# Layer 0's first MLP product as seven block products, its result by way of DRAM

## The chip, the cores and the metric

The kernel runs on one core of a Trainium2 chip. A core has five engines with instruction streams of their own: TensorE (PE; its weight loads are listed apart as PEld), VectorE (DVE), ScalarE (ACT), GpSimd (POOL) and SyncE (SP), which here only issues transfers. The metric is the device time of one execution in microseconds (us), lower is better.

## The reference, cut to what matters

Two layers run over 512 latent tokens and 256 context tokens of width 1024, all in float32. Per layer:

```
u   = modulate(rmsnorm(x, norm1_w), sh1, sc1)
z   = split(u @ w_in)                       # 5888 columns: retention, attention, pooling, gates
mix = merge_branches(retention, pooling, attention, gates, ...) @ w_out
x   = x + g1 * mix
x   = x + g2 * (square(relu(modulate(rmsnorm(x, norm2_w), sh2, sc2) @ w_mlp1)) @ w_mlp2)

pooling: mixed = einsum('blgc,gcd->blgd', window_means - ug, w_grp) * scale     # 4 groups of 128 channels
```

`w_mlp1` is 1024 x 4096, `w_mlp2` 4096 x 1024. Layer 0 computes all 768 tokens (6 tiles of 128), the last layer only the 512 latent ones after its projections.

## The kernel before, in words

**Products.** Each float32 operand is split into a high part (rounded to float32r by a ScalarE copy) and a low part (the rest, by a subtraction on VectorE or GpSimd). `mm3` (L302 to L305) then issues three matmuls: high x high, high x low, low x high. Almost all TensorE work goes through these three lines, so the profile's groups are told apart by the tile that they write: `tg` (projections, output projection, last MLP chunks), `pg` (gates), `pb` (branches), `pu` (pooling projection), `pp` (pooling mix), `ph` (first MLP product), `st` (second MLP product).

**Weights.** The class `Weights` holds one plan of slots in the order of their use. `next` hands out slot i, issues the loads of slot i+3 on SP's queue (L109) and enters the split of slot i+2 in a list; `tick`, called between matmuls, takes one piece of 512 columns from that list (L139 on ScalarE, L140 on VectorE or GpSimd). There are six raw buffers and three pairs of split ones. `combine` (L152) adds or subtracts two raw blocks on GpSimd, for the second MLP product.

**Order.** Work is written as generators that are interleaved by hand: a `Filler` gives out so many estimated microseconds of matmuls between the steps of a chain of dependent work. A scheduler then orders each engine's instructions by a simulated time line, so that a ready instruction can go ahead of an earlier one that waits. Large tiles (12 KB a partition) come from one pool, `big`, of 11 buffers.

**Layer 0 in time.** From 0 to some 150 us: modulation weights, norm, and the first projections (`T1`: pairs of 256 columns, moving operand 256 wide). To 320 us: the other projections (`T2`) as filler beside retention and the query and key norms; the four pooling groups come last. Each group's `pu` is evicted to `up` (one buffer), VectorE adds shifted copies (`ps`), forms `pd`, and the mixing matmul `pp` (`mixed`, L693) is issued after the next group's first eviction; the result goes to `pm`. To 620 us: attention, with the gates and branches 0 and 1 as filler; `to_hilo_feat` splits `pm` before branch 1. To 759 us: branch 2 and the output projection, in two groups of tiles, (0,1,2,3) and (4,5), each followed by its part of the second norm. To 1290 us: the MLP, with layer 1's modulation products between.

**The MLP.** The 4096 hidden columns are 8 chunks of 512. The first product of a chunk (`mlp1`, L1244) runs slab by slab of 128 hidden columns, moving 512 and then 256 tokens, 8 k-tiles x 3 matmuls each; ScalarE makes relu and square in place (L1263, L1264). Chunks 0 to 5 then go through `strassen` (L1169), the second product as seven block products of 2 x 2 blocks (Strassen-Winograd): VectorE forms sums of blocks of the hidden state (L1191), ScalarE and VectorE split them (L1195, L1196), and each of the 21 banks of a chunk is added to the sums `acc` (L1225; in chunk 0 twelve of them are copied by ScalarE). The order is m1 0, then m1 c and s2 c-1 in turn, s2 5, `fold`, m1 6, m1 7, and `m2` for chunks 6 and 7 in the ordinary way:

```python
            o = [("m1", 0)]
            for ch in range(1, NSC):
                o += [("m1", ch), ("s2", ch - 1)]
            o += [("s2", NSC - 1), ("fold",), ("m1", 6), ("m1", 7)]
```

Layer 1 has the same form with 512 tokens.

## Time and profile before

| | |
|---|---|
| median of 3 runs | 2161.41 us (2160.17 to 2162.72) |
| profiled execution | 2159.42 us, of it 2157.6 us from the first to the last instruction |
| TensorE busy, mean granted clock | 2091.7 us (97%), 0.992 |
| VectorE, ScalarE, GpSimd busy | 1323.2, 860.0, 614.9 us |
| read from and written to memory | 216.27 MB, 7.37 MB |

The trace is of one execution. A matmul's duration in it reaches past the start of the next one, since they are pipelined; starts show the rate. A window's row gives each engine's busy time in a stretch, with the number of instructions in brackets.

### The profile page before, as it was taken

What the parts mean: (1) busy time and instruction counts of PE and PEld (TensorE: products, weight loads), DVE (VectorE), ACT (ScalarE), POOL (GpSimd) and SP (SyncE); (2) the same over time, 40 slices, a digit from 0 to 9 for tenths busy, and PEclk for the clock granted to TensorE, in tenths of its full rate; (3) what the DMA queues carried; (4) which work ended last, traced back from release to release, by engine and by line L of the source; (5) the groups of instructions that cost most, each with busy time, mean ns of one, the idle gap of its engine ahead of it and who ended that gap; (6) DMA issues with size and microseconds to landing.
All of it is one profiled execution on the core that took longest, in us unless ns stands there. A gap on an engine that the chain in (4) does not pass through costs nothing.

```text
span 2157.6 us, 33841 instructions
## 1 busy us (share of the span) xinstructions
PE 2091.7 (97%) x13407; PEld 1803.8 (84%) x13407; DVE 1323.2 (61%) x2523; ACT 860.0 (40%) x1707; POOL 614.9 (29%) x481
## 2 busy tenths in 40 slices
PE   5999989999999999999999999998999999999999
PEld 5999968888888788888888889996888888887787
DVE  4597973454543654446569557479455367778884
ACT  3323423443432354434343335233454445654441
POOL 0242242222223331232222224333333353212300
PEclk8999999999999999999999999999999999999999
DMA  9751111111124534244426243211222164233241
GB/s 314 241 174 40 41 38 55 50 40 50 40 59 161 155 135 146 91 135 128 139 96 206 69 146 101 79 46 51 74 61 77 54 209 128 88 98 111 80 132 49
DMA packets 224598, 225.83 MB, mean 105 GB/s; under 512 B 8320, under 2 KB 180664, under 8 KB 224440
## 3 DMA queue, kind: packets, MB, share of 16 engines
q1 hardware_dynamic: 208744, 168.96, 25.3%
q0 software_dynamic: 15696, 54.71, 7.3%
q8 instruction: 105, 1.72, 0.3%
q14 instruction: 53, 0.43, 0.1%
HBM read 216.27 MB, written 7.37 MB: 104 GB/s over the span
## 4 chain that ended last, share of the span: by engine, by line
PE 81%; DVE 13%; issue 2%; ACT 2%; DMA 1%; POOL 0%; SPq 0%; DVEq 0%; ACTq 0%; POOLq 0%
PE ph L303 7%; PE ph L304 7%; PE ph L305 7%; PE tg L304 5%; PE tg L303 5%; PE tg L305 5%; PE pg L303 5%; PE pg L305 5%; PE pg L304 5%; PE st L303 4%; PE st L304 3%; PE st L305 3%; PE pb L304 3%; PE pb L303 3%; PE pb L305 3%; PE m L1099 2%
## 5 line engine op out<-in xcount | busy, mean ns | idle before, releaser
L140 POOL TENSOR_TENSOR wl<-wr,wh 128x512 fp32r<-128x512 f32 x304 | 415.2, 1379 | 938.8 <-ACT wh L139 904.3
L139 ACT ACTIVATE wh<-wr 128x512 fp32r<-128x512 f32 x640 | 370.6, 623 | 556.8 <-issue 222.1
L140 DVE TENSOR_TENSOR wl<-wr,wh 128x512 fp32r<-128x512 f32 x336 | 238.1, 731 | 254.9 <-ACT wh L139 254.8
L304 PE MATMUL ph<-u2l,wh 128*128 128x512 f32 (+1 forms) x808 | 278.9, 346 | 1.3 <-DVE u2l L1379 1.3
L303 PE MATMUL ph<-u2h,wh 128*128 128x512 f32 (+1 forms) x808 | 279.3, 348 | 0.3 <-ACT wh L139 0.3
L305 PE MATMUL ph<-u2h,wl 128*128 128x512 f32 (+1 forms) x808 | 277.4, 345 | 0.0
L303 PE MATMUL tg<-wh,uh 128*128 128x256 f32 x784 | 226.6, 289 | 1.0 <-ACT uh L1378 0.9
L304 PE MATMUL tg<-wl,uh 128*128 128x256 f32 x784 | 223.7, 285 | 1.6 <-POOL wl L140 1.6
L305 PE MATMUL tg<-wh,ul 128*128 128x256 f32 x784 | 222.6, 285 | 0.0
L303 PE MATMUL pg<-uh,wh 128*128 128x512 f32 (+1 forms) x576 | 208.4, 362 | 0.0
L304 PE MATMUL pg<-ul,wh 128*128 128x512 f32 (+1 forms) x576 | 207.1, 360 | 0.0
L305 PE MATMUL pg<-uh,wl 128*128 128x512 f32 (+1 forms) x576 | 207.1, 359 | 0.0
L152 POOL TENSOR_TENSOR wr<-wr,wr 128x1024 f32<-128x1024 f32 x48 | 116.7, 2430 | 259.1 <-DVE wl L140 220.0
L303 PEld LDWEIGHTS ph<-u2h,wh 128*128 128x128 f32 x808 | 152.1, 189 | 22.4 <-issue 2.8
L303 PE MATMUL st<-wh,ob 128*128 128x512 f32 x420 | 165.6, 398 | 5.1 <-DVE acc L1225 2.9
L304 PEld LDWEIGHTS ph<-u2l,wh 128*128 128x128 f32 x808 | 153.0, 189 | 19.9 <-DVE u2l L1379 1.7
L305 PEld LDWEIGHTS ph<-u2h,wl 128*128 128x128 f32 x808 | 152.8, 189 | 18.7
L304 PE MATMUL st<-wl,ob 128*128 128x512 f32 x420 | 165.2, 393 | 1.1 <-DVE wl L140 1.1
L305 PE MATMUL st<-wh,ob 128*128 128x512 f32 x420 | 164.7, 392 | 0.0
L303 PEld LDWEIGHTS tg<-wh,uh 128*128 128x128 f32 x784 | 150.8, 192 | 3.5 <-issue 1.8
L304 PEld LDWEIGHTS tg<-wl,uh 128*128 128x128 f32 x784 | 150.9, 193 | 2.7 <-POOL wl L140 2.0
L305 PEld LDWEIGHTS tg<-wh,ul 128*128 128x128 f32 x784 | 150.3, 192 | 1.3 <-issue 1.2
(316 smaller groups left out, 4160.4 us busy)
## 6 DMA issues: line engine op xcount, KB each, us to landing
wr<-in_w_mlp_dram SPq DMA_DIRECT2D x136, 512.0 KB, 4.2
wr<-in_w_in_dram SPq DMA_DIRECT2D x88, 512.0 KB, 3.8
adaw<-in_ada_w_dram POOLq DMA_DIRECT2D x42, 1024.0 KB, 6.1
wr<-in_w_out_dram SPq DMA_DIRECT2D x32, 512.0 KB, 3.9
adaw<-in_ada_w_dram SPq DMA_DIRECT2D x6, 1024.0 KB, 18.2
wr<-in_w_ret_out_dram SPq DMA_DIRECT2D x16, 256.0 KB, 2.8
wr<-in_w_pool_out_dram SPq DMA_DIRECT2D x16, 256.0 KB, 2.8
wr<-in_w_attn_out_dram SPq DMA_DIRECT2D x32, 128.0 KB, 3.0
```

What stands on the lines that cost most here:

```text
L139: A.activation(out=box["h"][:, a:b], in_=r[:, a:b], func=AF.Copy)
L140: eng.tensor_tensor(out=box["l"][:, a:b], in0=r[:, a:b], in1=box["h"][:, a:b].bitcast(F32), op=ALU.subtract)
L152: nc.gpsimd.tensor_tensor(out=t, in0=self.raw[a], in1=self.raw[b], op=f)
L303: T.matmul(ps, ah, bh, start=first, stop=False, **kw)
L304: T.matmul(ps, ah, bl, start=False, stop=False, **kw)
L305: T.matmul(ps, al, bh, start=False, stop=last, **kw)
L1099: T.matmul(m2[KV[v], 2, :], vt[:, b, 64 * v : 64 * v + 64], PT[:, v, i, :], start=(i == 0), stop=(i == nb - 1), tile_position=(0, 64 * v), ...
```

## The change

In layer 0 (`SA`), the first MLP product of all eight chunks becomes seven block products as well (`s1`): weights in blocks of 512 rows x 256 columns, tokens in halves of 384, so 4 k-tiles x 2 slabs x 3 matmuls of 384 columns for each product. The seven operands of the token side (`operands`) are formed once and kept in seven large tiles; the weight blocks' sums are formed on GpSimd in halves. Each chunk's hidden state is written to DRAM and read back for the second product, whose six chunks now follow all eight first products; chunks 6 and 7 are split when they come back (`split67`). The output projection of layer 0 goes in groups of three tiles.

The first projections (`t_wide`) put two neighbouring blocks of 256 columns beside each other, moving 512 columns. The pooling mix leaves the projection stage: VectorE writes `pd`'s values to `pm`, and `mix_gen` runs the mixing matmuls between branches 0 and 1 and splits their result; layer 0's groups go from the widest window to the narrowest; the first gate takes the place at the end of the projection stage. Layer 1 has the changes of projection and pooling, not that of the MLP. The core of the diff:

```diff
+    class Beside(tuple):
+        def __new__(cls, whole, parts):
+            t = super().__new__(cls, (whole,))
+            t.parts = parts
+            return t
...
+            if isinstance(src, Beside):
+                for q, sq in enumerate(src.parts):
+                    nc.sync.dma_start(out=r[:, :].rearrange("p (k b n) -> p k b n", k=k, b=2)[:, :, q, :], in_=sq)
+                self.raw[name] = r
+                return
...
+                for op in pre[1] if pre is not None else ():
+                    self.bg.append((i, lambda op=op: self.combine(*op)))
-                eng = V if key[0] == "s2" or key[0] in ("m1", "m2") and not (key[0] == "m1" and key[1:3] == (1, 0) and key[3] > 1) or key[:2] == ("t", 0) and key[2] < C_AK else nc.gpsimd
+                eng = V if key[0] in ("s1", "s2") or key[0] in ("m1", "m2") and not (key[0] == "m1" and key[1:3] == (1, 0) and key[3] > 1) or key[:2] == ("t", 0) and key[2] < C_AK else nc.gpsimd
+                half = key[0] == "out" or key[0] in ("m1", "m2") and key[1] == 0 or key[:3] == ("t", 0, C_RV + 256) or key[0] == "s1" and key[3] > 1
...
+        def combine(self, o, a, b, f, oo=0, ao=0, bo=0, n=1024):
+            if o not in self.raw:
+                self.raw[o] = wp.tile([P, 1024], F32, name=f"wr{self.nr}", tag="raw", bufs=6)
+                self.nr += 1
+            nc.gpsimd.tensor_tensor(out=self.raw[o][:, oo : oo + n], in0=self.raw[a][:, ao : ao + n], in1=self.raw[b][:, bo : bo + n], op=f)
...
-    T2 = ((C_RG, C_RG + 256, C_AK, C_AQ, C_AQ + 256, 0, 1, 2, 3), (C_RG, C_RG + 256, C_AK, 3, 2, C_AQ, C_AQ + 256, 1, 0))
+    T2 = ((C_RG, C_RG + 256, C_AK, C_AQ, C_AQ + 256, 3, 2, 1, 0), (C_RG, C_RG + 256, C_AK, 3, 2, C_AQ, C_AQ + 256, 1, 0))
...
+    ON = (((0, 1, 2), (3, 4, 5)) if 0 in SA else NG[0], NG[1])
...
+        if l in SA:
+            o = [("s1", ch) for ch in range(8)] + [("s2", ch) for ch in range(NSC - 1)] + [("h67",), ("s2", NSC - 1), ("fold",)]
+            return o + [("m2", 6, g) for g in (NG[0] if l == 0 else mlp2_groups(l, 6))]
...
-            kp = t1_kper(l, pr)
-            for s in range(KT // kp):
-                for cb in pr:
-                    W.add(("t", l, cb, s), wslab(w_in[l], s * kp * P, kp, cb, 256))
+            for s in range(KT // 2):
+                q = [wslab(w_in[l], s * 256, 2, cb, 256) for cb in pr]
+                W.add(("t", l, pr[0], s), Beside(wslab(w_in[l], s * 256, 2, 0, 512), q))
...
+            if o[0] == "s1":
+                slab = [wslab(w_mlp1[l], 0, 8, o[1] * CHUNK + j * P, P) for j in range(4)]
+                r0, r1, ra = ([(l, o[1], n, q) for q in range(2)] for n in ("r0", "r1", "ra"))
+                add, sub = ALU.add, ALU.subtract
+                for q in range(2):
+                    W.add(("s1", l, o[1], q), slab[0], ([(r0[q], slab[2 * q])], []), parts=((r0[q], 0), (r0[q], 512)))
+                for q in range(2):
+                    ops = [(ra[q], r1[q], r1[q], add, 0, 0, 512, 512), (ra[q], ra[q], r0[q], sub, 512, 0, 0, 512)]
+                    W.add(("s1", l, o[1], 2 + q), slab[0], ([(r1[q], slab[2 * q + 1])], ops), parts=((ra[q], 0), (ra[q], 512)))
+                for q in range(2):
+                    ops = [(r1[q], r0[q], r1[q], sub, 0, 0, 0, 512), (r0[q], r0[q], ra[q], sub, 512, 512, 512, 512)]
+                    W.add(("s1", l, o[1], 4 + q), slab[0], ([], ops), parts=((r1[q], 0), (r0[q], 512)))
+                W.add(("s1", l, o[1], 6), slab[0], ([], []), parts=((r1[0], 512), (r1[1], 512)))
...
+        def t_wide(pr):
+            short = [t for t in alltiles if pr[1] >= C_RQ and t not in tiles]
+            banks = {}
+            sv = [store(dsts[cb]) for cb in pr]
+            for s in range(KT // 2):
+                wh, wl = W.next(("t", l, pr[0], s))
+                for t in alltiles:
+                    n = 256 if t in short else 512
+                    o = 256 * short.index(t) if t in short else 0
+                    key = -1 if t in short else t
+                    if key not in banks:
+                        banks[key] = ps.tile([P, 512], F32, name=f"tw{t}", tag="g")
+                    for k in range(2):
+                        kk = 2 * s + k
+                        tt = slice(t * P, (t + 1) * P)
+                        mm3(banks[key][:, o : o + n], xh(kk)[:, tt], xl(kk)[:, tt], wh[:, k, :n], wl[:, k, :n],
+                            first=(kk == 0 and o == 0), last=(kk == KT - 1), skip_group_check=True)
+                    if 2 * s + 2 == KT:
+                        if t not in short:
+                            for q in range(2):
+                                sv[q](banks[t][:, 256 * q : 256 * q + 256], [t])
+                        elif t == short[-1]:
+                            sv[0](banks[-1], short)
+                    W.tick()
+                    yield 2 * 3 * n / 2400.0
+
+        f1 = Filler(chainup(*[t_wide(pr) for pr in T1]))
...
-                d = wk.tile([P, 800], F32, name=f"pd{g}", tag=f"pls{(g + 1) % 2}")
-                V.scalar_tensor_tensor(out=d[:, 8:e], in0=src[:, 8:e], scalar=1.0 / w, in1=up[:, 8:e], op0=ALU.mult, op1=ALU.subtract)
...
+                    d = pm[:, g, t0 : t0 + n]
+                    V.scalar_tensor_tensor(out=d, in0=src[:, o : o + n], scalar=1.0 / w, in1=up[:, o : o + n], op0=ALU.mult, op1=ALU.subtract)
...
-                def mixed(g=g, d=d, pw=pw):
-                    for t0, n in groups:
-                        o = 8 if t0 == 0 else 536
-                        pp = ps.tile([P, 512], F32, name=f"pp{g}{t0}", tag="r")
-                        T.matmul(pp[:, :n], pw, d[:, o : o + n], start=True, stop=True)
-                        A.activation(out=pm[:, g, t0 : t0 + n], in_=pp[:, :n], func=AF.Copy, scale=wcol[l][:, 64 + g : 65 + g])
-                pend.append(mixed)
...
-            while pend:
-                pend.pop(0)()
+            y_tile()
+            yield from gate(0, 0, y_part(0))
...
+        pw = wkt.tile([P, 4, P], F32, name=f"pw{l}", tag="th")
+        nc.gpsimd.dma_start(out=pw, in_=pool_w[l].rearrange("g k d -> k g d"))
+
+        def mix_gen():
+            bh, bl = hl["p"] = bigt(f"bph{l}", F32R), bigt(f"bpl{l}", F32R)
+            for g in range(4):
+                sc = wcol[l][:, 64 + g : 65 + g]
+                for t0, n in groups:
+                    pp = ps.tile([P, 512], F32, name=f"pp{g}{t0}", tag="g")
+                    T.matmul(pp[:, :n], pw[:, g, :], pm[:, g, t0 : t0 + n], start=True, stop=True)
+                    h = bh[:, g, t0 : t0 + n]
+                    A.activation(out=h, in_=pp[:, :n], func=AF.Copy, scale=sc)
+                    V.scalar_tensor_tensor(out=bl[:, g, t0 : t0 + n], in0=pp[:, :n], scalar=sc, in1=h.bitcast(F32), op0=ALU.mult, op1=ALU.subtract)
+                    yield 4 * n / 2400.0
...
+                elif b == 0:
+                    ths = y_part(ft)
+                    if ft:
+                        yield from gate(b, ft, ths)
...
-        f3 = Filler(chainup(branch_gen(0, lambda: hl["r"]), branch_gen(1, lambda: to_hilo_feat(pm, "bp")), gate2_gen()))
+        f3 = Filler(chainup(branch_gen(0, lambda: hl["r"]), mix_gen(), branch_gen(1, lambda: hl["p"]), gate2_gen()))
...
+        def operands(part):
+            ublk = lambda kh, th: u2h[kh][:, :, th * HT : th * HT + HT]
+            b11, b12, b21, b22 = (ublk(kh, th) for kh in range(2) for th in range(2))
+            for pq, blk, sm in ((1, b11, None), (2, b21, None)) if part == 0 else (
+                    (5, b11, (b12, b11)), (6, b11, (b22, b11)), (7, b12, (b22, b12)), (3, b22, None), (4, b21, (b21, b11))):
+                o = big.tile([P, 2, 4, HT], F32R, name=f"ub{l}{pq}", tag="big")
+                ub[pq] = o
+                for k in (slice(0, 2), slice(2, 4)):
+                    if sm:
+                        V.tensor_tensor(out=blk[:, k], in0=sm[0][:, k], in1=sm[1][:, k], op=ALU.subtract)
+                    A.activation(out=o[:, 0, k], in_=blk[:, k], func=AF.Copy)
+                    V.tensor_tensor(out=o[:, 1, k], in0=blk[:, k], in1=o[:, 0, k].bitcast(F32), op=ALU.subtract)
+
+        hd = [tc.dram_tile([P, 4 * ntok], F32, name=f"hd{l}{ch}") for ch in range(8)] if sa else None
+
+        def s1(ch):
+            ht = big.tile([P, 4, ntok], F32, name=f"ht{l}{ch}", tag="big")
+            banks = {}
+            seq = [[(1, 0), (2, 0)], [(1, 1), (2, 1)], [(5, 0), (6, 0)], [(5, 1), (6, 1)], [(7, 0), (3, 0)], [(7, 1), (3, 1)], [(4, 0), (4, 1)]]
+            for e, prods in enumerate(seq):
+                wh, wl = W.next(("s1", l, ch, e))
+                for hf, (pq, q) in enumerate(prods):
+                    key = {1: "x", 6: "x", 7: "x", 4: "x", 5: "y", 3: "y", 2: "z"}[pq], q
+                    new = key not in banks
+                    if new:
+                        banks[key] = ps.tile([P, 512], F32, name=f"sp{l}{ch}{pq}{q}", tag="g")
+                    bk = banks[key][:, :HT]
+                    for k in range(4):
+                        mm3(bk, wh[:, 4 * hf + k, :], wl[:, 4 * hf + k, :], ub[pq][:, 0, k], ub[pq][:, 1, k], new and k == 0, k == 3, skip_group_check=True)
+                        if k % 2:
+                            W.tick()
+                    f, th = {1: (0, 0), 2: (0, 0), 5: (1, 1), 6: (0, 1), 7: (1, 1), 3: (0, 1), 4: (1, 0)}[pq]
+                    hv = ht[:, 2 * q + f, th * HT : th * HT + HT]
+                    if pq in (1, 5, 6, 4):
+                        A.activation(out=hv, in_=bk, func=AF.Copy)
+                    else:
+                        V.tensor_tensor(out=hv, in0=bk, in1=hv, op=ALU.add)
+                    if pq in (3, 4):
+                        hf2 = ht[:, 2 * q + f, :]
+                        V.scalar_tensor_tensor(out=hf2, in0=hf2, scalar=0.0, in1=hf2, op0=ALU.max, op1=ALU.mult)
+                    yield 4 * 3 * HT / 2400.0
+                if ch == 0 and e == 1:
+                    yield None
+            nc.sync.dma_start(out=hd[ch], in_=ht.rearrange("p a b -> p (a b)"))
+
+        def load_h(ch):
+            if sa and ch not in hs:
+                hs[ch] = big.tile([P, 4, ntok], F32, name=f"hr{l}{ch}", tag="big")
+                nc.sync.dma_start(out=hs[ch].rearrange("p a b -> p (a b)"), in_=hd[ch])
+
+        def split67():
+            for ch in (6, 7):
+                load_h(ch)
+            for ch in (6, 7):
+                r = hs[ch]
+                hh, hl_ = bigt(f"hh{l}{ch}", F32R), bigt(f"hl{l}{ch}", F32R)
+                hs[ch] = (hh, hl_)
+                for j in range(4):
+                    A.activation(out=hh[:, j, :ntok], in_=r[:, j, :], func=AF.Copy)
+                    V.tensor_tensor(out=hl_[:, j, :ntok], in0=r[:, j, :], in1=hh[:, j, :ntok].bitcast(F32), op=ALU.subtract)
+                    yield 0.0
 
         def strassen(ch):
+            if sa:
+                load_h(ch)
+                load_h(ch + 1)
...
-        for q, gr in enumerate(NG[l]):
+        for q, gr in enumerate(ON[l]):
             for cb in range(2):
                 for _ in t_gemm(("out", l, gr, cb), yhk, ylk, KT, 2, 512, gr, ps, "g", resid(g1, cb)):
                     pass
             if q == 1:
                 early()
             norm_group(gr, [xr[t // 3][:, t % 3, :] for t in gr], cl[:, 3], cl[:, 2], u2h, u2l, wk, ps, "t")
-        early()
+            if sa:
+                operands(q)
+        if not sa:
+            early()
...
-        for i in range(0, len(ts), 2):
+        for i, j in ((0, 1), (1, 3)) if ts == (3, 4, 5) else [(i, i + 2) for i in range(0, len(ts), 2)]:
...
             for q in range(4):
-                norm_mod(ts[i : i + 2], xns[i : i + 2], q, a, sh, uh, ul, wk, psp, tag)
+                norm_mod(ts[i:j], xns[i:j], q, a, sh, uh, ul, wk, psp, tag)
```

## Rows read from the trace of the kernel before

**Rows 1.** The page: busy us, share and instructions of each engine

```profile
PE 2091.7 (97%) x13407; PEld 1803.8 (84%) x13407; DVE 1323.2 (61%) x2523; ACT 860.0 (40%) x1707; POOL 614.9 (29%) x481
```

**Rows 2.** Windows: length, busy us of PE, PEld, DVE, ACT, POOL, clock, DMA, GB/s

```profile
0.00:60.00 60.00, 37.21 (x331) 32.81 (x332) 24.26 (x93) 23.08 (x39) 4.98 (x10) 0.89 0.92 308
...
110.00:160.00 50.00, 48.48 (x572) 46.65 (x565) 46.10 (x87) 10.51 (x21) 23.62 (x27) 1.00 0.52 171
...
770.00:1200.00 430.00, 430.00 (x2899) 362.74 (x2898) 254.53 (x355) 173.24 (x314) 118.34 (x89) 1.00 0.40 129
```

**Rows 3.** Waits of PE: total us, times, longest

```profile
PE pp L697 <- DVE pd L691: 9.1, 2, 8.1
PE pp L697 <- issue: 7.9, 1, 7.9
...
PE st L303 <- DVE acc L1225: 2.9, 4, 0.8
...
PE pp L697 <- DVE qsT L761: 1.2, 1, 1.2
```

**Rows 4.** Timeline of PE, 259 to 267 us: start, us, instruction, tiles, shapes

```profile
259.22 0.40 PE L303 MATMUL pu<-uh,wh 128*128 128x512 f32 x1
...
263.76 0.39 PE L305 MATMUL pu<-uh,wl 128*128 128x512 f32 x1
...
264.10 0.28 PE L304 MATMUL pu<-ul,wh 128*128 128x256 f32 x1
...
266.74 0.28 PE L305 MATMUL pu<-uh,wl 128*128 128x256 f32 x1
```

**Rows 5.** PE groups by shape: busy us, mean ns, idle before

```profile
L303 PE MATMUL ph<-u2h,wh 128*128 128x512 f32 x472 | 185.2, 392 | 0.3 <-ACT wh L139 0.3
...
L304 PE MATMUL ph<-u2l,wh 128*128 128x256 f32 x336 | 94.9, 284 | 1.3 <-DVE u2l L1379 1.3
```

**Rows 6.** Timeline of DVE, 1137 to 1169 us

```profile
1151.78 0.94 DVE L1196 TENSOR_TENSOR ob<-hb,ob 128x768 fp32r<-128x768 f32 x1
1152.64 1.28 DVE L140 TENSOR_TENSOR wl<-wr,wh 128x512 fp32r<-128x512 f32 x2
1153.85 1.87 DVE L1225 TENSOR_TENSOR acc<-st,acc 128x512 f32<-128x512 f32 x3
```

**Rows 7.** POOL groups by shape, 800 to 1200 us

```profile
L152 POOL TENSOR_TENSOR wr<-wr,wr 128x1024 f32<-128x1024 f32 x23 | 55.7, 2421 | 88.7 <-DVE wl L140 53.4 <-issue 34.6
```

**Rows 8.** DMA issues, 770 to 1200 us: count, KB each, median us to landing

```profile
xq<-xk SPq DMA_DIRECT2D x6, 512.0 KB, 7.0
```

**Rows 9.** DVE groups by shape, 800 to 1200 us

```profile
L1196 DVE TENSOR_TENSOR ob<-hb,ob 128x768 fp32r<-128x768 f32 x24 | 25.8, 1077 | 18.6 <-ACT ob L1195 18.6
L1196 DVE TENSOR_TENSOR ob<-stt,ob 128x768 fp32r<-128x768 f32 x18 | 23.4, 1301 | 16.2 <-ACT ob L1195 16.1
```

**Rows 10.** Window of the `st` tile alone: PE, PEld, DVE, ACT, clock, DMA

```profile
1105.70:1169.00 63.30, 58.98 (x252) 46.48 (x252) 25.69 (x39) 0.00 (x0) 1.00 0.58 183
```

**Rows 11.** Windows of all engines in second-product stretches, layer 0 and layer 1

```profile
1137.00:1169.00 32.00, 32.00 (x201) 25.76 (x200) 31.97 (x44) 10.94 (x19) 8.57 (x9) 1.00 0.80 247
2018.70:2041.00 22.30, 18.38 (x76) 13.62 (x75) 21.71 (x28) 12.35 (x22) 7.92 (x3) 0.97 0.07 26
```

**Rows 12.** Timeline of DVE, 705 to 785 us, around the second norm

```profile
763.61 0.68 DVE L1154 TENSOR_TENSOR xr<-xr,rt 128x512 f32<-128x512 f32 x1
...
779.93 1.29 DVE L1379 TENSOR_TENSOR u2l<-un,u2h 128x512 fp32r<-128x512 f32 x2 [1.16 <-ACT u2h L1378]
```

**Rows 13.** Timeline of DVE, 255 to 300 us

```profile
281.03 6.49 DVE L840 TENSOR_TENSOR aq<-aq,ropeA 128x512 f32<-128x512 f32 x1
...
291.75 0.68 DVE L840 TENSOR_TENSOR aq<-aq,ropeA 128x512 f32<-128x512 f32 x1
```

**Rows 14.** Windows of all engines behind two waits for `pp`

```profile
296.00:303.00 7.00, 7.00 (x24) 4.95 (x23) 4.37 (x10) 2.23 (x5) 1.83 (x2) 0.79 0.16 47
...
1497.00:1510.00 13.00, 13.00 (x48) 9.51 (x47) 12.79 (x22) 2.56 (x5) 3.17 (x3) 0.87 0.14 40
```

More of the change, by code (lines that the diff above doesn't have):

```diff
@@ L193, in bslab @@
         return (v[0], v[1])
-    def t1_kper(l, pr):
-        return 2 if l == 0 and pr == T1[0] else 4
     def tslots(l, key, cb, kh):
@@ L240 @@
                 W.add(("br", l, b, ft), bslab(l, b, ft))
-        for gr in NG[l]:
+        for gr in ON[l]:
             for cb in range(2):
@@ L255 @@
                                           (4, [], (t4, b21, t2, sub), t4)):
-                    W.add(("s2", l, o[1], pq), q[0][0], (loads, op), of)
+                    W.add(("s2", l, o[1], pq), q[0][0], (loads, [op] if op else []), of)
             elif o[0] == "m1":
@@ L598, in layer @@
         alltiles = list(range(NT))
-        def tspec(cb, dst):
-            return (("t", l, cb), tiles if cb >= C_RQ else alltiles, store(dst))
         def tcol(cb, dst):
-            return t_multi([tspec(cb, dst)], xh, xl, KT, 4, 256, ps, "g")
+            return t_multi([(("t", l, cb), tiles if cb >= C_RQ else alltiles, store(dst))], xh, xl, KT, 4, 256, ps, "g")
         def rope_ret(dst):
@@ L652, in pool_gen @@
                 up = wk.tile([P, 800], F32, name=f"up{g}", tag="up", bufs=1)
-                pw = wk.tile([P, P], F32, name=f"pw{g}", tag="pw", bufs=2)
-                nc.gpsimd.dma_start(out=pw, in_=pool_w[l, g])
                 V.memset(up[:, 0:8], 0.0)
-                e = 520 if last else 792
                 V.memset(up[:, 520:536], 0.0)
@@ L910, in post_gen, with gate, y_tile, y_part @@
             yield from norm_q()
+        def gate(b, ft, ths):
+            gh, gl = W.next(("gate", l, b, ft))
+            for (t0, n), th in zip(groups, ths):
+                pg = ps.tile([P, 512], F32, name=f"pg{ft}{t0}", tag="g")
+                for k in range(KT):
+                    mm3(pg[:, :n], gh[:, k, :], gl[:, k, :], xh(k)[:, t0 : t0 + n], xl(k)[:, t0 : t0 + n], k == 0, k == KT - 1)
+                    if k % 4 == 3:
+                        W.tick()
+                        yield 4 * 3 * n / 2400.0
+                A.activation(out=th, in_=pg[:, :n], func=AF.Tanh, scale=0.5)
+        y = []
+        def y_tile():
+            y.append(bigt(f"y{l}{len(y)}"))
+        def y_part(ft):
+            return [y[ft // 4][:, ft % 4, t0 : t0 + n] for t0, n in groups]
         marks = set()
@@ L943, in layer @@
         wk = es.enter_context(tc.tile_pool(name=f"wk_a{l}", bufs=2, reuse_waits="tile"))
-        def to_hilo_feat(src, nm):
-            bh, bl = bigt(f"{nm}h{l}", F32R), bigt(f"{nm}l{l}", F32R)
-            for k in range(4):
-                A.activation(out=bh[:, k, :ntok], in_=src[:, k, :ntok], func=AF.Copy)
-                V.tensor_tensor(out=bl[:, k, :ntok], in0=src[:, k, :ntok], in1=bh[:, k, :ntok].bitcast(F32), op=ALU.subtract)
-            return bh, bl
+        pw = wkt.tile([P, 4, P], F32, name=f"pw{l}", tag="th")
[11 more added lines that the diff above has]
+                    yield 4 * n / 2400.0
         def to_hilo_att(nm):
@@ L959, in to_hilo_att @@
             return bh, bl
-        y = [bigt(f"y{l}{q}") for q in range(2)]
-        def gate(b, ft, ths):
-            gh, gl = W.next(("gate", l, b, ft))
-            for (t0, n), th in zip(groups, ths):
-                pg = ps.tile([P, 512], F32, name=f"pg{ft}{t0}", tag="g")
-                for k in range(KT):
-                    mm3(pg[:, :n], gh[:, k, :], gl[:, k, :], xh(k)[:, t0 : t0 + n], xl(k)[:, t0 : t0 + n], k == 0, k == KT - 1)
-                    if k % 4 == 3:
-                        W.tick()
-                        yield 4 * 3 * n / 2400.0
-                A.activation(out=th, in_=pg[:, :n], func=AF.Tanh, scale=0.5)
+        y_tile()
         th2 = []
@@ L1158, in layer @@
         ylk = lambda k: yl[k // 4][:, k % 4, :]
-        u2h = [bigt(f"u2h{l}{q}", F32R) for q in range(2)]
-        u2l = [bigt(f"u2l{l}{q}", F32R) for q in range(2)]
+        sa = l in SA
+        if sa:
+            u2h, u2l = [bigt(f"uf{l}{q}") for q in range(2)], None
+        else:
+            u2h = [bigt(f"u2h{l}{q}", F32R) for q in range(2)]
+            u2l = [bigt(f"u2l{l}{q}", F32R) for q in range(2)]
         u2hk = lambda k: u2h[k // 4][:, k % 4, :]
@@ L1293, in mlp_gen @@
                     yield from strassen(o[1])
+                elif o[0] == "s1":
+                    yield from s1(o[1])
+                elif o[0] == "h67":
+                    yield from split67()
                 elif o[0] == "fold":
```

66 lines of the change are left out of this document (31 added, 35 removed).

## The prediction

> **What bounds the kernel now.** I read the engine totals first: TensorE is busy 97% of the span, VectorE 61% [rows 1]. So only work taken from TensorE, or a stall of it, can shorten the time; then the stretches by window say where that holds. In layer 0's MLP (770 to 1200 us) TensorE is busy 430.00 of 430 us at full clock while VectorE has 254.5 [rows 2]: each product removed there is time gained, as long as nothing else becomes the bound. Before that, from 110 to 160 us, VectorE is busy 46.1 of 50 [rows 2], so TensorE time saved there is worth less. The list of what TensorE waits for is short, and the pooling product `pp` leads it: 9.1 us on VectorE's `pd`, 7.9 us on "issue" [rows 3].
>
> A matmul's price is the spacing of starts, not its printed duration, since matmuls overlap. Twenty 512-column matmuls after the one at 259.22 another starts at 263.76: 0.227 us each; twenty-two after 264.10 one starts at 266.74: 0.120 us for 256 columns [rows 4].
>
> **First MLP product of layer 0.** The groups of `ph` matmuls [rows 5] hold both layers. By the code, layer 0 has 720 matmuls of 512 columns and 864 of 256 (the first two slabs of chunk 0 go in three pieces of 256): 720 x 0.227 + 864 x 0.120 = 267.1 us. After: 8 chunks x 7 products x 2 slabs x 4 k-tiles x 3 = 1344 matmuls of 384 columns. No row has that width; it costs at least 0.120 and at most 0.227 [rows 4], and I take the middle, 0.1735, since 256 columns more cost 0.107: 233.2 us. **-33.9 us**; the two ends (161 and 305 us) would need a price that is not linear, so I keep 0.170 (three quarters of 0.227) to 0.180 for the range, -38.6 to -25.2. The Trainium skill ("TensorE: Matmul & The Clock Gate", Back-to-back issue gap) gives columns over 2.4 GHz plus 2.5 ns; by it the saving would be an estimated 31.3 us, 2.6 less, but its 215.8 ns for 512 columns is below the 227 here.
>
> Who else works during it, per chunk of 168 x 0.1735 = 29.1 us: VectorE 9 halves of weight splits and 6 evictions at 0.60, 4 squared ReLUs of 768 elements at 0.86 [rows 6] = 12.4 us; GpSimd 8 combinations of 512 (half of the 2.42 of a 1024 one [rows 7]) and 5 split halves, some 16 us. Neither bounds. The hidden state goes out over SP's queue, 1.5 MB a chunk, three times a 512 KB transfer that lands in 7.0 us when queued with others [rows 8]; weight loads queue behind it. Slots run three loads ahead, so I charge only **+2 us** for seven chunk ends (range 0 to 20).
>
> **Second product, now six chunks in a row.** This is the part that gives time back. A Strassen chunk of the second product in layer 0 has 126 matmuls of 512 columns: 28.6 us. VectorE does 21 evictions and 14 split halves at 0.60 (three evictions in 1.87 us, the last one 0.67 long) and 11 operations on 768 elements at 0.86 (1151.78 to 1152.64) [rows 6]: 30.5 us; the 768 ones average 1.08 and 1.30 rather than 0.94 [rows 9], about 0.23 each lost, so 33.1. Before, each such chunk stood beside a first-product chunk that needed VectorE little. Where two stood back to back (252 matmuls in 63.30 us, 31.65 a chunk [rows 10]), VectorE was busy 31.97 of the last 32 us and TensorE just kept up [rows 11]; in layer 1, whose second-product chunks are smaller, two in a row do stop TensorE: 18.38 of 22.30 us [rows 11], waiting for `acc` [rows 3]. The 31.65 are 3.0 above 28.6, which the next layer's modulation matmuls took. The filler units put about 40% of that work into the new six-chunk phase, so TensorE needs about 30.3 us a chunk and VectorE 33.1: 6 x 2.8 = 17, minus 7.2 (chunk 0 copies 12 banks on ScalarE), plus 6.9 for splitting chunks 6 and 7 (8 x 0.86), minus about 6 that six PSUM banks and the operands prepared ahead absorb: **+10 us**, range 0 (no hold-ups, 30.5) to 25 (no slack). The read-backs of the hidden state are prefetched one chunk ahead and need buffers that the block operands release during chunk 7; for the two handovers (into this phase, and `h67`, which wants six of eleven large buffers) **+2 us**, 0 to 12.
>
> **Into the MLP.** Output projection in groups (0,1,2), (3,4,5): same matmuls. Before, the last residual addition starts at 763.61 and the last low half of the norm at 779.93 [rows 12]: 17 us, of which 96 matmuls of 256 columns (11.5 us) cover the most and some 5 stay open. After, the last group has three tiles, the seven-product's first four half-slab products cover 48 x 0.1735 = 8.3 us, and behind the norm comes operand 5 (subtract, copy, subtract on VectorE and ScalarE, some 3 us) before TensorE can go on: **+6 us**, 0 to 12. VectorE's later operands (6, 7, 3, 4) keep pace with 4.1 us a slot.
>
> **Projection.** 256-column pairs become 512-column matmuls: layer 0, 576 x 0.120 to 288 x 0.227 = -3.7; layer 1, 528 x 0.120 to 240 x 0.227 + 48 x 0.120 = -3.1. Layer 0's part lies beside a nearly full VectorE [rows 2], so I take **-5**, -3 to -6.8. Each slot is now two 256 KB loads, so 512 KB more weights stand on SP's queue ahead of the start's modulation weights, in a stretch whose DMA engines are 92% busy at 308 GB/s [rows 2]: **+1.5 us**, 0 to 2.5 (768 KB).
>
> **Pooling.** The mixing product leaves the projection stage, so TensorE no longer stands at `pp`. In layer 0 the 9.1 us have a cause that stays: VectorE's queue, where one rope multiply takes 6.49 us instead of 0.68 [rows 13], and `up` has one buffer, so the next group's eviction, and by the third group TensorE's bank, wait for the same chain, now longest first. After such a wait the clock is low: 0.79 granted over 296 to 303, 0.87 over 1497 to 1510 [rows 14], of the levels 1.2 and 2.4 GHz, so 1.5 and 1.7 us more. Layer 0: **-6** (0 to -10.6). Layer 1's 7.9 plus clock plus a 1.2 us wait: there all pool products are already issued, and `gate(0, 0)` has 24 matmuls, 5.4 us, to run meanwhile: **-10** (-6 to -11). The product itself, the gate and the 16 `pp` matmuls only move: 0, covered by nothing, because TensorE executes them either way; the hi/lo split of `pm` on ScalarE and VectorE (16 operations) falls away off the path.
>
> **Sum:** -33.9 + 2 + 10 + 2 + 6 - 5 + 1.5 - 6 - 10 = -33.4. The profiled execution took 2159.4 us (span 2157.6 and 1.8 around it), so 2126.0; the median of the runs is 2.0 above that execution, so **2128 us**.
>
> **Rivals.** What a measurement can tell from no change is 0.2%, 4.3 us.
>
> A, the sum as it stands, 2112 to 2140: 0.58.
>
> B, VectorE never bounds and both pooling waits vanish whole: -33.9 - 6.8 - 10.6 - 11 + 6 + 2 = -54.3, 2107 us. For it speaks that TensorE lost nothing from 1137 to 1169 [rows 11]; against it that this was two chunks and not six: 0.10.
>
> C, VectorE bounds fully (+25 for +10) and layer 0's pooling wait stays (0 for -6): -12.4, 2149 us; 2140 to 2155: 0.18. Layer 1's row speaks for it.
>
> D, slower: the trip through DRAM. If each of 8 stores and 7 later reads of 1.5 MB stops TensorE, because the weights behind it on SP's queue are late, the gain is gone at (33.4 + 2)/15 = 2.4 us a transfer; at 5 us each, less than the 7.0 of a third of such a transfer [rows 8], it is +75 on a sum of -35.4: 2201 us. Against it: loads run three slots (12 us) ahead and memory stores of the residual passed earlier without a stop. 0.07.
>
> E, slower: GpSimd holds VectorE. One multiply took 6.49 for 0.68 [rows 13]. Were each of the 24 combinations of the second product to stop VectorE for its whole 2.42 us [rows 7], a chunk would cost it 30.5 + 9.7 = 40.2 against 30.3: 6 x 9.9 less the same 6 of slack = 53 instead of 10, and 2171 us. Measured, a chunk lost 2.6 rather than 9.7: 0.04. The Trainium skill ("SBUF — State Buffer", SBUF: two separate sides) says just this, that the port pair the two share is an exclusive lock, held for a whole instruction; the 6.49 agrees, the means [rows 9] show that it is seldom the full price.
>
> No change that can be measured: 0.03, between C and D. So faster 0.86, same 0.03, slower 0.11. Range 2104 to 2152: A, nearly all of C, and most of B.
>
> **What would show it.** Right: starts of the 384-column matmuls 0.17 to 0.18 us apart; no `pp` wait in the projection stage; VectorE above 95% busy and TensorE below 97% in the six-chunk phase, waiting for `acc`, `wl` or `ob`; an idle stretch of some 10 us at the norm before the first product. Wrong: a spacing well off 0.1735; TensorE waits at chunk ends for `wr` or `hr` loads (D); TensorE full through the six chunks (B); VectorE operations of 768 elements near 2 us (E). The weakest steps are the two that rest on no row of their own, the handovers and the norm seam.

## The result, and the profile after

The changed kernel takes 2175.76 us (median of 4 runs, 2174.99 to 2176.68) beside 2160.79 of the kernel before on the same chip: ratio 1.0072 [1.0054, 1.0089], 15 us slower where 33 us faster were forecast, outside the range. Its profiled span is 2174.7 us.

The page: engine totals, and what was moved to and from memory.

```profile
PE 2077.5 (96%) x12639; PEld 1776.7 (82%) x12639; DVE 1459.3 (67%) x2652; ACT 862.4 (40%) x1704; POOL 741.3 (34%) x547
...
HBM read 228.85 MB, written 19.96 MB: 114 GB/s over the span
```

Against [rows 1], TensorE has 768 matmuls less and only 14 us less busy time; VectorE has 136 us more, GpSimd 126. So TensorE lost time. What it waits for (total us, times, longest), which answers to [rows 3]:

```profile
PE ada L387 <- DMA adaw<-in_ada_w_dram: 11.9, 5, 5.2
PE st L330 <- DVE acc L1351: 11.5, 16, 3.0
PE pu L330 <- ACT up L714: 9.5, 1, 9.5
PE xt L1502 <- DVE xn L1491: 7.3, 3, 7.0
...
PE pb L330 <- ACT y L957: 5.9, 2, 5.2
PE ada L378 <- DVE acc L349: 5.2, 1, 5.2
```

No `pp` is left in it, as forecast. But `pu` now waits 9.5 us where `pp` waited 9.1, `pb` 5.2 where `pp` waited 7.9, and two lines lie for the most part in layer 0's MLP: the modulation weights `adaw` (8.1 of the 11.9 us) and the accumulator `acc` (8.5 of 11.5).

The MLP of layer 0 runs from the first `ph` or `sp` matmul to the first one of the last two chunks (`tg`): 759.1 to 1238.1 before, 479.0 us; 753.6 to 1262.1 after, 508.5 us. The seven-product form should have taken 14 us from it and added 29.5. Its three parts, as windows (length, busy us of PE, PEld, DVE, ACT, POOL, clock, DMA share, GB/s): the norm with the first 50 `sp`, the first phase (`s1`), the second (`s2`).

```profile
753.60:779.00 25.40, 16.09 (x76) 13.24 (x74) 21.32 (x41) 13.06 (x25) 9.58 (x11) 0.74 0.51 167
779.00:1038.50 259.50, 250.26 (x1751) 239.62 (x1751) 170.36 (x170) 93.98 (x174) 162.67 (x116) 0.97 0.52 171
1038.50:1262.10 223.60, 206.48 (x1108) 154.07 (x1108) 217.60 (x286) 90.23 (x147) 72.39 (x42) 0.98 0.49 174
```

What each part needs comes from spacings. The 384-column matmuls, in TensorE's timeline (start, duration):

```profile
830.56 0.33 PE L331 MATMUL sp<-ub,wh 128*128 128x384 f32 x1
...
833.87 0.33 PE L332 MATMUL sp<-ub,wl 128*128 128x384 f32 x1
```

Nineteen starts in 3.31 us: 0.174 each, where 0.1735 was taken. The 512-column ones stay at 0.227 [rows 4], and the 800 modulation matmuls took 25.8 us by the spacing of their starts before, 0.032 each. So:

| part | length | work at these prices | lost |
|---|---|---|---|
| norm | 25.4 | 50 x 0.174 + 24 transposes, some 2.5 = 11.2 | 14.2 |
| first phase | 259.5 | 1282 x 0.174 + 464 x 0.032 = 237.9 | 21.6 |
| second phase | 223.6 | 756 x 0.227 + 12 x 0.174 + 336 x 0.032 = 184.5 | 39.1 |

Before, the same sum is 267.1 (first product) + 171.6 (second) + 25.8 (modulation) + 3.8 (32 transposes) = 468.3 of 479.0: 10.7 us lost. The work fell by 34.7 us, about as forecast; the losses rose by 64.2, where 20 were forecast (2 + 10 + 2 + 6). The experiments are about these losses, and about the pooling.

### The profile page after: what moved, and what is told of

Read it like the earlier page. It is cut to its first block, busy times and chain, and to the rows that moved or that the text cites. A ratio compares the mean times of both kernels' runs of the same rounds, so it can differ in the third digit from the quotient of the medians.

```text
span 2174.7 us, 32623 instructions
## 1 busy us (share of the span) xinstructions
PE 2077.5 (96%) x12639; PEld 1776.7 (82%) x12639; DVE 1459.3 (67%) x2652; ACT 862.4 (40%) x1704; POOL 741.3 (34%) x547
## 4 chain that ended last, share of the span: by engine, by line
PE 67%; DVE 20%; DMA 5%; issue 4%; ACT 2%; POOL 1%; SPq 1%; DVEq 0%; POOLq 0%; ACTq 0%
PE pg L330 5%; PE pg L331 5%; PE pg L332 5%; PE tg L331 4%; PE tg L330 4%; PE tg L332 4%; DVE wl L154 3%; DMA adaw<-in_ada_w_dram 3%; PE pb L331 3%; PE pb L330 3%; PE ph L332 3%; PE ph L331 3%; PE pb L332 3%; PE ph L330 3%; PE sp L330 2%
## 5 line engine op out<-in xcount | busy, mean ns | idle before, releaser
L165 POOL TENSOR_TENSOR wr<-wr,wr 128x512 f32<-128x512 f32 (+1 forms) x96 | 206.5, 2165 | 278.8 <-DVE wl L154 260.9
L330 PE MATMUL st<-wh,ob 128*128 128x512 f32 x420 | 168.0, 406 | 16.1 <-DVE acc L1351 11.5
L330 PE MATMUL sp<-ub,wh 128*128 128x384 f32 x448 | 153.6, 348 | 3.6 <-DVE ht L1266 3.3
L331 PE MATMUL sp<-ub,wh 128*128 128x384 f32 x448 | 152.8, 341 | 0.1
L332 PE MATMUL sp<-ub,wl 128*128 128x384 f32 x448 | 152.1, 340 | 0.8 <-DVE wl L154 0.8
L330 PEld LDWEIGHTS pg<-uh,wh 128*128 128x128 f32 x576 | 108.9, 189 | 15.6 <-issue 1.4
L332 PEld LDWEIGHTS pg<-uh,wl 128*128 128x128 f32 x576 | 108.8, 189 | 15.5 <-issue 1.2
L330 PE MATMUL tg<-wh,uh 128*128 128x256 f32 x416 | 120.9, 291 | 0.0
L331 PEld LDWEIGHTS pg<-ul,wh 128*128 128x128 f32 x576 | 108.9, 189 | 14.4 <-issue 1.0
L331 PE MATMUL tg<-wl,uh 128*128 128x256 f32 x416 | 118.2, 284 | 0.0
L331 PE MATMUL ph<-u2l,wh 128*128 128x512 f32 (+1 forms) x280 | 103.5, 371 | 0.3 <-DVE u2l L1514 0.3
L330 PE MATMUL ph<-u2h,wh 128*128 128x512 f32 (+1 forms) x280 | 103.0, 372 | 0.3 <-ACT wh L153 0.3
## 6 DMA issues: line engine op xcount, KB each, us to landing
hd<-ht SPq DMA_DIRECT2D x8, 1536.0 KB, 12.2
```

What stands on the lines that cost most here:

```text
L165: nc.gpsimd.tensor_tensor(out=self.raw[o][:, oo : oo + n], in0=self.raw[a][:, ao : ao + n], in1=self.raw[b][:, bo : bo + n], op=f)
L330: T.matmul(ps, ah, bh, start=first, stop=False, **kw)
L331: T.matmul(ps, ah, bl, start=False, stop=False, **kw)
L332: T.matmul(ps, al, bh, start=False, stop=last, **kw)
```

## The experiments

Times are medians beside the kernel before in the same group of runs; ratios are to it. Its medians in the four groups lie between 2159.66 and 2160.79 us, so a difference between two groups is uncertain by about 1 us more.

**1. Projection and pooling alone** (both MLPs as before).

```diff
-SA = (0,)
+SA = ()
```

> The wide projection and the pooling change alone; layer 0's MLP as in the kernel before. Read from the changed kernel's trace, its stretches outside layer 0's MLP are 5.5 us (before it) and 6.9 us (after it) shorter than before. Theory: all of the loss lies in the MLP change, so this is about 12 us faster than before, some 2149 us (ratio 0.994). Rival: those gains were themselves an effect of the MLP change's other schedule, or the projection costs time too: ratio 0.999 or more.

2147.89 us against 2159.66, ratio 0.9944 [0.9929, 0.9958]. The rest of the change gains 11.8 us (21 less 1.5 had been forecast), so the seven-product form costs 15.0 + 11.8, some 27 us here, each beside its own kernel before.

**2. The output projection's old groups**, four tiles and then two, to put more work beside the norm.

```diff
-    ON = (((0, 1, 2), (3, 4, 5)) if 0 in SA else NG[0], NG[1])
+    ON = NG
```

> As the changed kernel, but the output projection of layer 0 in groups of four and two tiles as before, so that only two tiles are normed behind the last product. Theory: the norm of three tiles lengthens the idle stretch ahead of the block products (some 17 us from 762 to 779, with the clock at half until 783): 5 to 8 us faster than the changed kernel, some 2168 to 2171 us. Rival: the operands' VectorE chain sets that stretch whatever the group: within 2 us of 2176.

2181.05 us, ratio 1.0096 [1.0081, 1.0111]: 5 us slower than the change, not faster. TensorE's waits from 740 to 800 us:

```profile
PE xt L1502 <- ACT uf L1506: 7.0, 5, 2.8
PE sp L330 <- ACT ub L1240: 3.8, 2, 2.7
```

The block halves of 384 tokens are three tiles, so with four tiles first the operands of the second half come no sooner; the steady run of `sp` begins at 784.0 us rather than 779.0. The theory on this seam fell, and so did its rival, by which nothing would have changed.

**3. More of the second phase's splits on GpSimd** (the second half of each weight split).

```diff
-half = ... or key[0] == "s1" and key[3] > 1
+half = ... or key[0] == "s1" and key[3] > 1 or key[:2] == ("s2", 0)
```

> As the changed kernel, but the second half of each weight split of layer 0's second product goes to GpSimd. Theory: VectorE bounds the six chunks, so 7 splits of 0.6 to 0.8 us less a chunk give 25 to 33 us less VectorE work, of which at least 10 to 20 us show: 2156 to 2166 us. Rival: TensorE waits there for something else, or GpSimd's extra work blocks VectorE as much as it relieves it: 2172 us or more.

2189.95 us, ratio 1.0143 [1.0126, 1.016]: 14 us slower than the change, though VectorE had 42 operations less. Its groups in the second phase (busy us, mean ns):

```profile
L154 DVE TENSOR_TENSOR wl<-wr,wh 128x512 fp32r<-128x512 f32 x41 | 42.0, 1024 | 0.1
L1322 DVE TENSOR_TENSOR ob<-stt,ob 128x768 fp32r<-128x768 f32 x16 | 30.5, 1907 | 0.4 <-ACT ob L1321 0.4
...
L1317 DVE TENSOR_TENSOR stt<-hr,stt 128x768 f32<-128x768 f32 x5 | 11.2, 2235 | 0.0
```

What is taken from VectorE comes back as longer operations on it, as the rival said: from 1048 to 1272 us it is busy for 217.34 of 224.00 us, and TensorE waits 18.7 us for `acc` in the MLP where it waited 8.5.

**4. The modulation products later**: none in the first phase, all twelve in the second.

```diff
+            if sa:
+                fm.adv(211.0)
...
-                fm.adv(10.0)
+                fm.adv(4.5 if sa else 10.0)
```

> As the changed kernel, but layer 2's modulation products (24 blocks of 32 matmuls, some 1 us each) are laid into the second product's phase alone. Theory: in the first phase TensorE loses 8 us to their loads (which wait for a buffer that the hidden state's store holds) and some 5 us to the low clock after that; in the second phase they fill time in which VectorE holds TensorE up. So 15 to 25 us faster than the changed kernel: 2151 to 2161 us. Rival: the loads cost as much in the second phase, or VectorE does not bound it: 2170 us or more.

2152.62 us, ratio 0.9966 [0.9953, 0.9979]: 23 us faster than the change. Its two phases:

```profile
779.00:1005.90 226.90, 225.34 (x1283) 223.53 (x1282) 174.09 (x162) 96.33 (x178) 159.48 (x95) 0.99 0.40 130
1005.90:1237.70 231.80, 216.79 (x1577) 165.65 (x1575) 216.17 (x295) 90.49 (x147) 87.08 (x60) 0.97 0.63 232
```

The first phase, now of 1282 products alone (223.1 us), loses 4 us rather than 21.6. The second takes in 464 more modulation matmuls, 14.8 us of work, and grows by only 8.2: TensorE had room there, VectorE's 216 us did not change.

**5. Without the block sums** of the hidden state.

```diff
+            if sa:
+                pre, raw = {}, {**raw, 5: blk(1, 0), 6: blk(0, 0), 3: blk(0, 1), 7: blk(1, 1)}
```

> Left out: the four sums of hidden-state blocks a chunk that VectorE makes for layer 0's second product (24 operations on 768 elements; single blocks take their place, so TensorE, ScalarE, GpSimd and the transfers do what they did). Theory, VectorE bounds the six chunks: at 1.18 to 1.30 us for each of these operations in the changed kernel's profile 28 to 31 us of VectorE work go, and TensorE's own need there (some 185 of the 224 us) lets nearly all of it show: 20 to 30 us faster than the changed kernel, 2146 to 2156. Rival, the chunks wait for weights or read-backs and VectorE is full only because it is made to wait: under 6 us faster, above 2169.

2155.64 us, ratio 0.9977 [0.9967, 0.9987]: 20 us faster than the change, at the theory's edge. The second phase is 203.0 us, with VectorE at 193.09 where it had 217.60:

```profile
1038.50:1241.50 203.00, 195.46 (x1109) 153.76 (x1109) 193.09 (x262) 88.87 (x144) 70.06 (x42) 0.98 0.52 193
```

VectorE bounds that phase in the changed kernel: 24.5 us of its work go, and the phase gets 20.6 us shorter.

**6. Without the weight-block sums** on GpSimd.

```diff
+                    if l in SA:
+                        op, of = None, {5: b11, 6: b12, 7: b22, 4: b21}.get(pq, of)
```

> Left out: the four combinations of weight blocks a chunk that GpSimd makes for layer 0's second product (24 operations on 1024 elements, 2.65 us each; the loaded blocks are used in their place, so VectorE has the same operations on the same shapes). Theory, GpSimd's work stretches VectorE's: VectorE's operations in the six chunks get some 27 us shorter in sum (those on 768 elements from 1.2 to 1.3 back towards 0.9 us), and the run is 15 to 27 us faster than the changed kernel, 2149 to 2161. Rival, VectorE is full by its own count of operations: the means stay above 1.1 us, and the run is under 6 us faster, above 2169.

2151.42 us, ratio 0.9954 [0.9939, 0.9969]: 24 us faster than the change, with VectorE's operations untouched. VectorE's groups in the second phase, first of the changed kernel, then of this one:

```profile
L1351 DVE TENSOR_TENSOR acc<-st,acc 128x512 f32<-128x512 f32 x111 | 71.8, 677 | 2.9 <-PE st L332 2.9
L154 DVE TENSOR_TENSOR wl<-wr,wh 128x512 fp32r<-128x512 f32 x83 | 64.9, 807 | 0.1
L1322 DVE TENSOR_TENSOR ob<-hr,ob 128x768 fp32r<-128x768 f32 x23 | 29.0, 1261 | 0.0
L1322 DVE TENSOR_TENSOR ob<-stt,ob 128x768 fp32r<-128x768 f32 x17 | 20.4, 1199 | 0.0
```

```profile
L1353 DVE TENSOR_TENSOR acc<-st,acc 128x512 f32<-128x512 f32 x111 | 73.2, 682 | 12.5 <-PE st L334 12.5
L154 DVE TENSOR_TENSOR wl<-wr,wh 128x512 fp32r<-128x512 f32 x83 | 54.3, 681 | 0.1
L1324 DVE TENSOR_TENSOR ob<-hr,ob 128x768 fp32r<-128x768 f32 x23 | 21.8, 947 | 0.0
L1324 DVE TENSOR_TENSOR ob<-stt,ob 128x768 fp32r<-128x768 f32 x16 | 15.2, 947 | 0.0
...
1039.70:1239.30 199.60, 198.56 (x1109) 151.59 (x1108) 185.64 (x282) 89.50 (x146) 11.58 (x17) 1.00 0.54 191
```

Counts equal but for one, shorter means: 0.13 us less for each split, 0.25 to 0.31 for each 768-element operation; the evictions, which read PSUM, keep theirs. The weight loads land as before (3.5 us in the median, 3.3 in the changed kernel), so transfers are not what changed. In its window of the second phase (last line) TensorE is busy 198.56 of 199.60 us, with one wait of 1.0 us, and VectorE has 185.64: TensorE is now the fuller of the two. By the prices above 184.5 us of it are work; where the other 15.1 go was not traced.

**7. The stores on another queue.**

```diff
-nc.sync.dma_start(out=hd[ch], ...)
+nc.scalar.dma_start(out=hd[ch], ...)
```

> The eight stores of the hidden state to DRAM go out over ScalarE's queue and no longer over SP's, ahead of the weight loads. Theory, the trip through DRAM costs TensorE little by the queue it uses: within 4 us of the changed kernel, the two waits for the modulation weights in the first phase (8 us) stay or only move. Rival (my rival D, smaller): the stores hold up what is behind them on SP's queue; weights land in 5 to 7 us again instead of 11, the modulation waits go, and the run is 8 to 13 us faster.

2172.49 us, ratio 1.0054 [1.0037, 1.007]: 3 us faster than the change. Transfers of the first phase (count, KB, median us to landing), of the changed kernel and then of this one:

```profile
wr<-in_w_mlp_dram SPq DMA_DIRECT2D x29, 512.0 KB, 10.9
adaw<-in_ada_w_dram POOLq DMA_DIRECT2D x13, 1024.0 KB, 11.5
hd<-ht SPq DMA_DIRECT2D x7, 1536.0 KB, 12.2
```

```profile
wr<-in_w_mlp_dram SPq DMA_DIRECT2D x29, 512.0 KB, 9.6
adaw<-in_ada_w_dram POOLq DMA_DIRECT2D x13, 1024.0 KB, 10.4
hd<-ht ACTq DMA_DIRECT2D x7, 1536.0 KB, 5.1
...
779.20:1029.90 250.70, 245.91 (x1751) 236.03 (x1751) 170.28 (x170) 92.91 (x174) 164.18 (x116) 0.99 0.53 177
1029.90:1257.50 227.60, 209.41 (x1109) 155.06 (x1108) 217.59 (x286) 90.64 (x147) 73.49 (x42) 0.97 0.47 171
```

Theory and rival were each half right. The time is the theory's; but the first phase got 8.8 us shorter and the waits for `adaw` fell from 11.9 us to 5.1 in all. The second phase grew by 4.0 and took half of it back, with VectorE at 217.59 us of work as before. The weights land in 9.6 us and not in 5 to 7, so the stores on their queue explain little of the 10.9.

**8. Late modulation and two buffers for `up`.**

```diff
-up = wk.tile(..., tag="up", bufs=1)
+up = wk.tile(..., tag="up", bufs=2)
...
-qsT = wk.tile(..., tag="qsT", bufs=2)
+qsT = wk.tile(..., tag="qsT", bufs=1)
```

> The late modulation products of the fourth run, and two buffers for the pooling's `up` (and one in place of two for the attention's `qsT`, to make room). Theory: with two `up` buffers TensorE no longer stands for 9.5 us in layer 0's pooling and keeps its clock (13.7 us at half clock go, some 6 us more): 9 to 16 us faster than the fourth run, 2137 to 2144. Rival: the wait comes from VectorE's queue (the chain of pooling sums behind the rope), and one more buffer only moves it to the next group or into attention: under 4 us faster, above 2148.

2146.75 us, ratio 0.9933 [0.9918, 0.9948]: 6 us faster than run 4, between theory and rival. `pu` still waits for `up`, 4.1 us where it was 9.5, so the buffer was part of the cause; the rest is VectorE's chain by the rival's account, which no run tested by itself.

```profile
PE pu L330 <- ACT up L714: 4.1, 1, 4.1
```

**9. Projection and pooling with two `up` buffers** (run 1 with the diff of run 8).

> The first run (projection and pooling alone) with two buffers for `up` (one for `qsT`). Theory: what the second buffer gave beside the seven-product form (6 us) it gives here too, since it lies in layer 0's projection stage, ahead of the MLP: 2139 to 2144, the fastest of all these kernels. Rival: without the first product's change the stage is no different, but the later MLP takes it back: above 2146.

2143.65 us against 2160.51, ratio 0.992 [0.9907, 0.9932], as the theory had it: the lowest median of all these kernels, and it has no seven-product form. Run 8 is 3 us above it, and their intervals overlap: with late modulation and two `up` buffers the seven-product form costs some 3 us over run 9, not 27.

**10. The pooling alone**: run 1 with the projection's old form put back.

```diff
-        f1 = Filler(chainup(*[t_wide(pr) for pr in T1]))
+        f1 = Filler(chainup(*[t_pair(pr) for pr in T1]))
```

(`t_pair` is the `t_multi` call of before, and the plan has its slots again.)

> The pooling's change alone: MLP and projection of the kernel before. Theory: layer 1's pooling product no longer stops TensorE (7.9 us and its half clock), but the tanh queue takes part of that (5.2 us wait for `y`), and layer 0's wait stays: 5 to 9 us faster than before; the other 3 to 7 of the first run's 12 are the projection's. Rival: the projection carries nearly all, pooling alone within 3 us of before.

2160.2 us, ratio 0.9999 [0.999, 1.0008]: no difference, so the theory fell and the rival holds; what run 1 gains comes with the projection, 11.5 us when each run is taken beside its own kernel before. The projection without the pooling's change was not run. The waits, first those of layer 0, then of layer 1:

```profile
PE pu L331 <- ACT up L719: 9.6, 1, 9.6
...
PE pb L331 <- ACT y L962: 5.2, 1, 5.2
```

**11. Three modulation products in the norm's gap** (run 8 with these moved).

```diff
+                if sa:
+                    layer_consts(l + 1, ...)
+                    nxt = chainup(*[ada(l + 1, v, c0, 512, ...) ...])
+                    for _ in range(9):
+                        next(nxt)
             norm_group(gr, ...)
```

> As the kernel with late modulation and two `up` buffers, but three of the twelve modulation products are put between the first half-slab products and the transposes of the second norm half, where TensorE stands for 7 us and then runs at half clock. Theory: the stand is for want of work, so three products (some 6 us of TensorE at full clock) fill it, the clock stays up, and the second phase has 6 us less: 5 to 10 us faster than that kernel, 2137 to 2142. Rival: their weights are not there, or their copies on VectorE stand ahead of the norm's, and the norm comes later by as much: within 3 us of it.

2162.41 us, ratio 1.0007 [0.9998, 1.0016]: 16 us slower than run 8, worse than the rival said. The largest wait of TensorE, and the transfers issued from 745 to 785 us:

```profile
PE lct L425 <- DMA lrows<-in_pool_scale_dram: 16.8, 1, 16.8
```

```profile
adaw<-in_ada_w_dram POOLq DMA_DIRECT2D x6, 1024.0 KB, 12.0
xk<-xr SPq DMA_DIRECT2D x3, 512.0 KB, 14.9
...
lrows<-in_pool_scale_dram POOLq DMA_DIRECT2D x1, 2.0 KB, 14.4
```

A row of 2 KB landed after 14.4 us beside 6 MB of modulation weights on the same queue and some 4 MB of other transfers. The wait is for the rows of `layer_consts`, which was moved together with the three products. The work was there to fill the gap; its data was not. Whether the products alone, or an earlier load, would do it was not tried.

## Why the prediction was wrong, step by step

The forecast was -33.4 us, the measured change +15.0. Three steps failed: the second product's +10, where VectorE's company with GpSimd was taken as 2.6 us a chunk and measured 5.3; the first phase's +2, which put the loads of the woven-in modulation products at nothing; and the pooling's -16, where the wait did not go but moved. The signs named for being right all appeared: a spacing of 0.174, no `pp` wait, VectorE 97% and TensorE 92% busy in the six chunks, a stand of 7.0 us at the norm. They show that the mechanism was there; they could not tell a loss of 10 us from one of 39.

**First product, -33.9: right.** Spacing 0.174; the work fell by what was forecast.

**Second product, +10: wrong, and the largest error.** The direction was right (VectorE full, TensorE waiting for `acc`, `ob` and `wl`), the size was not: 39.1 us are lost in that phase. The own need of VectorE was well counted: 30.5 us a chunk forecast, 185.64/6 = 30.9 when GpSimd's sums are away (run 6). So was TensorE's: 30.3 forecast, 184.5/6 = 30.8. What was undersized is the company of GpSimd: 2.6 us a chunk, put on the 768-element operations alone. It is (217.60 - 185.64)/6 = 5.3, since the weight splits are stretched too, and the 6 us of slack were not there: VectorE's 217.60 us lie 33.1 above TensorE's 184.5, and VectorE stood for another 6.0. Run 6 shows the cause (24 us), run 3 the same from the other side (14 us). Run 5, which takes work from VectorE and leaves GpSimd's, shows that VectorE is the bound (20 us). These shares are not to be added: either alone brings the phase to 200 or 203 us, where TensorE is 96 to 99% busy. The +2 for the handovers was not the error: VectorE waits 6.8 us for the first `hr` ahead of the phase, in run 6 as well (6.7), which loses 0.6 us in the first 15 of the phase where the changed kernel loses 6.6. What stops TensorE there, 3.3 us for `ht`, follows VectorE operations of 3.17 and 3.13 us on 768 elements beside GpSimd's sums, which take 0.95 in run 6.

**The first phase, +2: wrong by some 20 us, at a place that was not looked at.** Stores and weight loads were weighed, and TensorE hardly waits for those. The modulation products, priced at their matmuls and spread by the filler units, need 1 MB loads into the large buffers and beside the new stores. They landed in a median of 6.0 us before and in 11.5 after, and twice TensorE stood for them (5.2 and 2.5 us), each time with half the clock after it (0.50 and 0.53 granted). The landing before, and the first of the two windows:

```profile
adaw<-in_ada_w_dram POOLq DMA_DIRECT2D x22, 1024.0 KB, 6.0
...
919.50:926.30 6.80, 5.26 (x43) 4.79 (x44) 0.94 (x2) 1.35 (x3) 0.06 (x1) 0.50 1.07 344
```

Run 4 shows that without them the phase loses 4 us; run 7 that the queue of the stores makes up 8.8 of the 21.6. By the counts of matmuls at the prices above, the 15 us around each stand lose 8.1 and 4.2 us, of which 7.7 are the stands and the rest is mostly the low clock; the first 15 us of the phase, where the clock is still low from the norm (0.51 granted from 779 to 783), lose 3.2. Why the loads come late when the stores are on another queue, the buffers or the other transfers, was not separated.

**Into the MLP, +6 (to 12): somewhat low.** The loss around the norm went from some 5 us (25.9 us for 144 `ph` of 256 columns at 0.120 and 32 transposes, 3.8) to 14.2, +9. TensorE stands 7.0 us for `xn`, and the mean granted clock of that window is 0.74. The norm's own small operations on VectorE are held up there as well, beside two weight splits on GpSimd:

```profile
763.19 2.86 POOL L154 TENSOR_TENSOR wl<-wr,wh 128x512 fp32r<-128x512 f32 x2 [1.29 <-ACT wh L153]
...
763.62 1.23 DVE L325 TENSOR_TENSOR rsq_t<-rs 128x3 f32<-128x3 f32 x1
764.88 1.19 DVE L326 TENSOR_TENSOR rsq_t<-rsq_t,rsq_v 128x3 f32<-128x3 f32 x1
...
766.29 0.16 DVE L325 TENSOR_TENSOR rsq_t<-rs 128x3 f32<-128x3 f32 x1
```

**Projection, -5 and +1.5: low.** Run 10 against run 1 gives -11.5, each beside its own kernel before; -3.5 had been forecast. By the start of the MLP and the end of the two traces 7.3 lie in layer 0 and 5.1 in layer 1, beside counts of 3.7 and 3.1. In layer 0 TensorE's clock from 20 to 60 us is 0.96 in run 1 where it was 0.83; why the clock holds there, and where layer 1's other 2 us come from, was not tested.

**Pooling, -16: wrong; it is 0.** The warning in the text (layer 0's cause is VectorE's queue and the one `up` buffer) was the whole story of layer 0, and was discounted to -6. In layer 1 the cover that was named, `gate(0, 0)`, puts its tanh on ScalarE, which stands 3.4 us for VectorE's `KS` there and has three other operations first; `pb` waits 5.2 us for `y`, with the clock low again behind it. In both layers the wait took another name (windows of layer 0 and layer 1, both at a granted clock of 0.50):

```profile
277.80:291.40 13.60, 5.39 (x25) 5.39 (x26) 13.53 (x31) 0.90 (x3) 6.07 (x6) 0.50 0.19 42
1513.40:1520.20 6.80, 4.77 (x11) 3.80 (x12) 6.66 (x23) 1.88 (x4) 1.31 (x1) 0.50 0.39 114
```

**The sum as measured:** pooling 0, projection -11.5, seven-product form +27 (from runs 10 and 1, each beside its own kernel before): +15.

**The rivals.** E came nearest in time (2171) and named the engine. It priced the second phase at 53 us lost, each sum at its full length; 39.1 were lost, of which 24 go with GpSimd's sums. The rest of the slowdown came from the first phase, the seam and the pooling, so its nearness in time is in part chance. C had two mechanisms right, VectorE as the bound (+25) and layer 0's pooling wait that stays, but sized the first too low and had nothing for the first phase. The Trainium skill ("SBUF — State Buffer", SBUF: two separate sides) states that the shared port pair is an exclusive lock for a VectorE operation with two SBUF inputs against a GpSimd operation that reads SBUF. Run 6 agrees in both halves: the operations on two SBUF tiles shrink from 1.26 to 0.95 us, those with one input in PSUM stay at 0.68. As in the means before [rows 9], the full length of a GpSimd sum (2.67 us here) is not what each costs: 22 of them last 58.6 us and took 32 from VectorE.

```profile
L165 POOL TENSOR_TENSOR wr<-wr,wr 128x1024 f32<-128x1024 f32 x22 | 58.6, 2665 | 99.6 <-DVE wl L154 90.9 <-issue 7.7 <-POOL wr L165 0.7
```

D had the right transfers and the wrong victim: not the products, but the modulation weights beside them.
